# A seven-product form for 106 of 370 weight chunks of a decoder layer, with gate and up as one unit

## The chip, the cores and the metric

The kernel runs on one core of one Trainium2 chip. The metric is the time of one execution on the device in microseconds (us), the median of several runs. The engines are named as in the profile: PE is the matrix engine (PEld its weight loads), DVE the vector engine, ACT the scalar engine, POOL GpSimd, and SP issues the transfers.

## The reference

One decoder layer on 256 tokens of 2048 channels, in float32, with two SwiGLU feed-forwards of inner width 5632 around a mixer and an attention to a memory of 256 rows:

```
h = h + 0.5 * (silu(n @ w1_gate) * (n @ w1_up)) @ w1_down      n = rmsnorm(h) * g_ffn1
z = (rmsnorm(h) * g_mix) @ w_in                                 # 3072 columns, and 256 for keys and values
y = [rmsnorm(spatial gating of z), rmsnorm(attention over a window of 128)]
h = h + y @ w_out
h = h + (attention of 4 heads of 512 to rmsnorm(mem)) @ w_xo    # w_xq, w_xkv
h = h + 0.5 * (silu(n @ w2_gate) * (n @ w2_up)) @ w2_down
out = rmsnorm(h) * g_final
```

## The kernel before

Nearly all of the work is products of the 256 tokens' activations with weights that are streamed once. Tokens lie in two blocks of 128 (tb). A float32 operand is written as a sum of two values of the type float32r, hi + lo, and a product is the sum of three matmuls, hi·hi + hi·lo + lo·hi, into one PSUM bank.

**A chunk** of weights is 1 MB: [128, 4, 512], four 128-row tiles of a 512-column block. `unit` goes over the chunks of one block of 512 columns: SP loads `raw` (three buffers), ACT casts it to `wh`, DVE computes `wl = raw - wh` (two buffers each; `split`, L144 and L145), and PE runs 4 row tiles x 2 token blocks x 3 matmuls (L223 to L225) into two banks of the pool `acc`. The activations are the stationary operand (a transposed [128, 128] block, hi or lo), the weights are the moving one. There are 370 chunks (368 of this form, and two of 256 columns for keys and values).

**A feed-forward** (`ffn`) goes in three phases over 4, 4 and 3 of the 11 blocks of 512 inner columns. For each block there is a gate unit and an up unit (4 chunks each), then silu on ACT (L238), the product on DVE (L240), eight transposes on PE (L162) and the split of the result; after a phase come four down units, one for each 512 columns of h, which are added to h (L251). `next_norm` squares each finished block of h, transposes it and splits it with the next norm's gain (L138, L139); the token's factor rs is applied to the product's rows. The first norm's input comes transposed from the host (xT); x itself is loaded into h later, beside the first block.

**The other stages**: w_in by blocks of 512 columns, window attention (small matmuls) beside the memory's value units, the memory's key units, w_out, then for each head a w_xq unit and its attention, and w_xo. The order of instructions on each engine is made by the tile framework from priorities in the order of the program and from its estimate of when each is ready; an engine then runs its list in order, with semaphores.

Of the kernel before, what the change touches and what calls it, by code (L numbers as in the profile page):

```python
# [30 lines left out]
def layer_kernel(  # L31
# [82 lines left out]
    def rstd_of(parts, n, width, nt=TB):  # L114
        """(mean of squares + eps) ** -0.5 from parts [P, nt, n]."""
        ss = tiny.tile([P, nt], F32, tag="ss", name=nm("ss"))
        if n > 1:
# [6 lines left out]
        nc.gpsimd.tensor_tensor(rs, ms, mhalf[:, :nt], ALU.pow)
        return rs
# [25 lines left out]
    def group_from_rows(s, src, gcol=None, into=None):  # L151
        """Transposed (hi, lo) of 512 columns; src(tb, i) is the [P, 128] block i."""
        if into is None:
            hi, lo = pair(s)
        else:
            hi, lo = [into(s).rearrange("p (k t) -> p k t", k=4) for _ in range(2)]
        for half in range(2):
            ps = bank(s)
            pv = ps.rearrange("p (k t) -> p k t", k=2)
            for i in range(2):  # L160
                for tb in range(TB):
                    nc.tensor.transpose(  # L162
                        pv[:, i, tb * P:(tb + 1) * P], src(tb, 2 * half + i), ident
                    )
# [26 lines left out]
    def unit(s, w, cb, groups, order=None, r0=0, fills=None, apart=False):
# [6 lines left out]
        kt = w.shape[3]  # L198
        ncol = w.shape[4]
        n = len(groups) * 4 // kt  # L200
        ps = [acc.tile([P, 512], F32, tag="acc", name=nm(s)) for _ in range(TB)]
        for at, ci in enumerate(range(n) if order is None else order):
            raw = stream.tile([P, kt, ncol], F32, tag="raw", name=nm(s + "w"), bufs=3)
            wh = stream.tile([P, kt, ncol], F32R, tag="wh", name=nm(s + "wh"))
            wl = stream.tile([P, kt, ncol], F32R, tag="wl", name=nm(s + "wl"))
            step = kt if fills is None else 1 if at == 0 else 2
            for k in range(0, kt, step):
                ks = slice(k, k + step)
                if fills is not None:
                    fills[ci](k, step)  # L210
                nc.sync.dma_start(raw[:, ks, :], w[r0 + ci, cb, :, ks, :])
                split(wh[:, ks, :], wl[:, ks, :], raw[:, ks, :])
            steps = [(k, tb) for k in range(kt) for tb in range(TB)]
            if apart and at == n - 1:
                steps.sort(key=lambda step: step[1])
            for k, tb in steps:
                hi, lo = groups[(ci * kt + k) // 4]
                kg = k % 4
                sl = slice(tb * P, (tb + 1) * P)
                o = ps[tb][:, :ncol]  # L220
                first = at == 0 and k == 0
                last = at == n - 1 and k == kt - 1
                nc.tensor.matmul(o, hi[:, kg, sl], wh[:, k, :], start=first, stop=False)  # L223
                nc.tensor.matmul(o, hi[:, kg, sl], wl[:, k, :], start=False, stop=False)  # L224
                nc.tensor.matmul(o, lo[:, kg, sl], wh[:, k, :], start=False, stop=last)  # L225
        return ps

    def ffn(s, groups, rs, wg, wu, wd, on_block, fills=None, apart=False):
        for p0, p1 in ((0, 4), (4, 8), (8, 11)):
            acts = []  # L230
            for c in range(p0, p1):
                pg = unit(s + "g", wg, c, groups, fills=None if c else fills)
                pu = unit(s + "u", wu, c, groups)
                if callable(rs):
                    rs = rs()
                sg = [s2("sg") for _ in range(TB)]
                for tb in range(TB):
                    nc.scalar.activation(sg[tb], pg[tb], AF.Silu, scale=rs[:, tb:tb + 1])  # L238
# [447 lines left out]
```

## Time and profile before

| what | value |
|---|---|
| runs | 2148.64, 2148.91, 2149.71 us (median 2148.91) |
| profiled execution | span 2147.1 us; the runs' median is 1.8 us more, which lies around the span |
| PE / DVE / ACT busy | 2132.2 / 1074.0 / 903.5 us |
| read from HBM | 398.52 MB, 187 GB/s over the span |
| granted TensorE clock | 0.999 |

Busy shares say how full an engine is, not what bounds; that is read from waits and from the chain that ended last. Matmuls overlap in the pipeline, so a matmul's own duration (some 390 ns) is longer than the distance of two starts.

### The profile page before, as it was taken

To read this page: it belongs to the slowest core of one execution; us is meant where nothing else is said; L and a number is where in the kernel's file an instruction comes from. 1 tells how busy PE (TensorE), PEld (TensorE's weight loads), DVE (VectorE), ACT (ScalarE), POOL (GpSimd) and SP (SyncE) were. 2 spreads that over 40 slices of the span, in tenths; PEclk is the share of its full clock that TensorE was granted. 3 is DMA by queue.
4 is the path that set the end of the run, shared out by engine and by line. 5 is a ranking of instruction groups with operands and counts; after the bars stand their busy time and mean duration, and the time that the engine had idled before them with its cause. 6 is when DMAs were issued, how large, how long until landed. Compare 5 with 4: busy or idle time off the path is not lost.

```text
span 2147.1 us, 22925 instructions
## 1 busy us (share of the span) xinstructions
PE 2132.2 (99%) x9782; PEld 1758.0 (82%) x9782; DVE 1074.0 (50%) x827; ACT 903.5 (42%) x841; POOL 16.7 (1%) x34
## 2 busy tenths in 40 slices
PE   9999999999999999999999999999999999999998
PEld 7888888888888888877888888888888888888886
DVE  5444444454445545555545555545444444544454
ACT  6333333333334455444434454443333343333333
POOL 0000000000000000000000000000000000000000
PEclk9999999999999999999999999999999999999999
DMA  8555555555555575434555534555555555555553
GB/s 296 194 192 184 195 194 190 184 194 196 196 179 195 191 251 202 162 116 157 176 187 186 178 143 169 176 194 184 191 191 190 190 193 188 187 194 196 186 188 136
DMA packets 61398, 402.10 MB, mean 187 GB/s; under 512 B 6752, under 2 KB 10864, under 8 KB 14192
## 3 DMA queue, kind: packets, MB, share of 16 engines
q1 hardware_dynamic: 60048, 396.44, 52.3%
q0 software_dynamic: 1248, 4.20, 0.6%
q8 instruction: 76, 1.25, 0.2%
q14 instruction: 26, 0.21, 0.0%
HBM read 398.52 MB, written 2.10 MB: 187 GB/s over the span
## 4 chain that ended last, share of the span: by engine, by line
PE 96%; DVE 1%; ACT 1%; DMA 1%; issue 0%; SPq 0%; POOL 0%; POOLq 0%; DVEq 0%; ACTq 0%
PE f2g L223 4%; PE f2u L224 4%; PE f2g L224 4%; PE f1d L223 4%; PE f2g L225 4%; PE f1d L225 4%; PE f1d L224 4%; PE f2u L223 4%; PE f2u L225 4%; PE f2d L223 4%; PE f2d L224 4%; PE f2d L225 4%; PE f1g L224 4%; PE f1g L225 4%; PE f1g L223 4%; PE f1u L225 4%
## 5 line engine op out<-in xcount | busy, mean ns | idle before, releaser
L145 DVE TENSOR_TENSOR f2uwl<-f2uw,f2uwh 128x2048 fp32r<-128x2048 f32 x44 | 100.9, 2293 | 138.6 <-ACT f2uwh L144 138.6
L145 DVE TENSOR_TENSOR f1uwl<-f1uw,f1uwh 128x2048 fp32r<-128x2048 f32 x44 | 100.9, 2293 | 138.0 <-ACT f1uwh L144 138.0
L145 DVE TENSOR_TENSOR f2gwl<-f2gw,f2gwh 128x2048 fp32r<-128x2048 f32 x44 | 100.9, 2293 | 114.2 <-ACT f2gwh L144 114.2
L145 DVE TENSOR_TENSOR f1dwl<-f1dw,f1dwh 128x2048 fp32r<-128x2048 f32 x44 | 100.9, 2293 | 112.5 <-ACT f1dwh L144 112.5
L145 DVE TENSOR_TENSOR f2dwl<-f2dw,f2dwh 128x2048 fp32r<-128x2048 f32 x44 | 100.9, 2293 | 111.2 <-ACT f2dwh L144 111.2
L145 DVE TENSOR_TENSOR f1gwl<-f1gw,f1gwh 128x2048 fp32r<-128x2048 f32 (+2 forms) x50 | 101.8, 2036 | 108.7 <-ACT f1gwh L144 108.5
L144 ACT CAST f2gwh<-f2gw 128x2048 fp32r<-128x2048 f32 x44 | 84.1, 1912 | 152.4 <-PE f2g L225 74.8
L144 ACT CAST f2dwh<-f2dw 128x2048 fp32r<-128x2048 f32 x44 | 84.2, 1913 | 151.5 <-PE f2d L225 123.3
L144 ACT CAST f1dwh<-f1dw 128x2048 fp32r<-128x2048 f32 x44 | 84.1, 1912 | 147.3 <-PE f1d L225 126.1
L144 ACT CAST f1gwh<-f1gw 128x2048 fp32r<-128x2048 f32 (+2 forms) x50 | 85.3, 1705 | 139.8 <-PE f1g L225 70.4
L224 PE MATMUL f1g<-f1gwl,n1h 128*128 128x512 f32 x352 | 138.1, 392 | 0.6 <-DVE f1gwl L145 0.5
L223 PE MATMUL f1g<-f1gwh,n1h 128*128 128x512 f32 x352 | 136.6, 390 | 1.8 <-ACT f1gwh L144 1.8
L224 PE MATMUL f2g<-f2gwl,n4h 128*128 128x512 f32 x352 | 137.9, 392 | 0.0
L225 PE MATMUL f1g<-f1gwh,n1l 128*128 128x512 f32 x352 | 137.7, 391 | 0.0
L225 PE MATMUL f2g<-f2gwh,n4l 128*128 128x512 f32 x352 | 137.7, 391 | 0.0
L224 PE MATMUL f1d<-f1dwl,f1ah 128*128 128x512 f32 x352 | 137.5, 391 | 0.0
L223 PE MATMUL f1d<-f1dwh,f1ah 128*128 128x512 f32 x352 | 137.3, 390 | 0.0
L225 PE MATMUL f1d<-f1dwh,f1al 128*128 128x512 f32 x352 | 137.3, 390 | 0.0
L224 PE MATMUL f2d<-f2dwl,f2ah 128*128 128x512 f32 x352 | 137.3, 390 | 0.0
L223 PE MATMUL f2g<-f2gwh,n4h 128*128 128x512 f32 x352 | 137.2, 390 | 0.0
L225 PE MATMUL f2d<-f2dwh,f2al 128*128 128x512 f32 x352 | 137.2, 390 | 0.0
L224 PE MATMUL f2u<-f2uwl,n4h 128*128 128x512 f32 x352 | 137.1, 389 | 0.0
(249 smaller groups left out, 4838.2 us busy)
## 6 DMA issues: line engine op xcount, KB each, us to landing
f1uw<-in_w_up SPq DMA_DIRECT2D x44, 1024.0 KB, 4.8
f1dw<-in_w_down SPq DMA_DIRECT2D x44, 1024.0 KB, 4.8
f2gw<-in_w_gate SPq DMA_DIRECT2D x44, 1024.0 KB, 4.8
f2uw<-in_w_up SPq DMA_DIRECT2D x44, 1024.0 KB, 4.8
f2dw<-in_w_down SPq DMA_DIRECT2D x44, 1024.0 KB, 4.8
f1gw<-in_w_gate SPq DMA_DIRECT2D x40, 1024.0 KB, 4.8
mvw<-in_w_xkv SPq DMA_DIRECT2D x16, 1024.0 KB, 4.8
mkw<-in_w_xkv SPq DMA_DIRECT2D x16, 1024.0 KB, 4.8
```

What stands on the lines that cost most here:

```text
L144: nc.scalar.copy(hi, src)
L145: nc.vector.tensor_tensor(lo, src, hi.bitcast(F32), ALU.subtract)
L223: nc.tensor.matmul(o, hi[:, kg, sl], wh[:, k, :], start=first, stop=False)
L224: nc.tensor.matmul(o, hi[:, kg, sl], wl[:, k, :], start=False, stop=False)
L225: nc.tensor.matmul(o, lo[:, kg, sl], wh[:, k, :], start=False, stop=last)
```

## The change

Two changes go together. First, **units are twice as wide**: a chunk is now 256 rows x 1024 columns (two row tiles k, two blocks j of 512 columns: gate and up of the same inner columns, or two neighbouring blocks of another matrix), still 1 MB as [128, 4, 512], and a unit fills four banks, one for each token block and column block. Seen as a product of 2 x 2 blocks, A (token block, row tile) times B (row tile, column block), a chunk takes eight block products of three matmuls. Second, **some chunks take seven** (Winograd's form of Strassen's product). There are three kinds of activation pair:

- N: eight plain products (mixer, memory);
- C: eight products, but into the sums that the seven-product form uses (banks P2, Q5, Q3, Q4), with two extra activation blocks S3 and S5;
- S: seven products, with sums S1 to S4 of activation blocks and T1 to T4 of weight blocks, into those banks and three more (P1, Q6, Q7, from the pool of transposes).

In a unit that mixes C and S, the results follow from the seven banks by DVE additions: one part after the last S chunk (`early`), one at the end. Kinds by chunk: CCSCSCSC for gate|up (11 units a feed-forward), w_out and w_xo (2 units each), CCSCSCSC CCSCCSC CCSCCSC for the 22 row pairs of down. That makes 106 S chunks; the other units (w_in, w_xq, w_xkv) use N.

`ffn` now runs all 11 gate|up units, keeps their 22 transposed results unsplit, and then runs down in four pieces: half 0 with pairs 0 to 7, half 1 with 0 to 14, half 0 with 8 to 21, half 1 with 15 to 21 (a half is 1024 columns of h). Sums and splits of a pair (`fill_sums`) are made when down first uses it. The first norm now comes from x: loaded in blocks of 512 columns, squared, scaled by an estimate of the factor from the first block, transposed on PE, and filled (`pre1`); the fourth norm is scaled by an estimate from half of h in the same way. Pairs have five slots for C and three for S.

```diff
@@ activations: a pair of row tiles
+    NAMES = {"N": ("A11", "A21", "A12", "A22"),
+        "C": ("A11", "A12", "A21", "A22", "S3", "S5"),
+        "S": ("A11", "A22", "A12", "S3", "S1", "S2", "S4")}
...
+    def fill_sums(s, p, raw):
+        f = s2(s + "f").rearrange("p (k t) -> p k t", k=4)
+        if p.kind == "C":
+            f = f[:, :2, :]
+            nc.vector.tensor_tensor(f, raw[:, 0:2, :], raw[:, 2:4, :], ALU.subtract)
+            split(p.hi[:, :4, :], p.lo[:, :4, :], raw)
+            split(p.hi[:, 4:, :], p.lo[:, 4:, :], f)
         else:
+            nc.vector.tensor_tensor(
+                f[:, 0:2, :], raw[:, 0:1, :].to_broadcast([P, 2, P]), raw[:, 1:3, :], ALU.subtract)
+            split(p.hi[:, :3, :], p.lo[:, :3, :], raw[:, 1:, :])
+            nc.vector.tensor_tensor(f[:, 2, :], raw[:, 1, :], f[:, 1, :], ALU.subtract)
+            nc.vector.tensor_tensor(f[:, 3, :], raw[:, 3, :], f[:, 2, :], ALU.subtract)
+            split(p.hi[:, 3:, :], p.lo[:, 3:, :], f)
@@ products of a chunk
+    MIXED = (("P2", ("A11", "B11"), ("A12", "B21")), ("Q5", ("A21", "B12"), ("A22", "B22")),
+        ("Q3", ("S3", "B12"), ("S5", "B22")), ("Q4", ("A21", "B11"), ("A22", "B21")))
+    SEVEN = (("P1", ("A11", "B11")), ("P2", ("A12", "B21")), ("Q3", ("S4", "B22")),
+        ("Q5", ("S1", "T1")), ("Q7", ("S3", "T3")), ("Q6", ("S2", "T2")), ("Q4", ("A22", "T4")))
...
+        def mm(self, name, a, b):
+            if name not in self.banks:
+                pool, tag = (trp, "tr") if name in ("P1", "Q6", "Q7") else (acc, "acc")
+                self.banks[name] = pool.tile([P, 512], F32, tag=tag, name=nm(self.s + name))
+            (ah, al), (bh, bl) = a, b
+            for x, y in ((ah, bh), (al, bh), (ah, bl)):
...
+        def chunk(self, w, p, pieces=False):
+            raw = stream.tile([P, 4, 512], F32, tag="raw", name=nm(s + "w"), bufs=3)
+            wh = stream.tile([P, 4, 512], F32R, tag="wh", name=nm(s + "wh"))
+            wl = stream.tile([P, 4, 512], F32R, tag="wl", name=nm(s + "wl"))
+            if p.kind == "S":
+                nc.sync.dma_start(raw, w)
+                t = stream.tile([P, 4, 512], F32, tag="t", name=nm(s + "t"), bufs=1)
+                th = stream.tile([P, 4, 512], F32R, tag="th", name=nm(s + "th"), bufs=1)
+                tl = stream.tile([P, 4, 512], F32R, tag="tl", name=nm(s + "tl"), bufs=1)
+                split(wh[:, 1:, :], wl[:, 1:, :], raw[:, 1:, :])
+                nc.vector.tensor_tensor(
+                    t[:, 0:2, :], raw[:, 1:3, :], raw[:, 0:1, :].to_broadcast([P, 2, 512]), ALU.add)
+                nc.vector.tensor_tensor(t[:, 2, :], t[:, 0, :], raw[:, 2, :], ALU.add)
+                nc.vector.tensor_tensor(t[:, 3, :], t[:, 2, :], raw[:, 3, :], ALU.add)
+                split(th, tl, t)
...
+            else:
+                nc.sync.dma_start(raw, w)
+                split(wh, wl, raw)
+            for name, *terms in PRODUCTS[p.kind]:
+                for an, bn in terms:
+                    self.mm(name, p[an], b[bn])
@@ combination (the first early is of gate|up, the second, made by add_early, of down, w_out and w_xo)
+    KINDS = "CCSCSCSC"
+    KINDS_D = "CCSCSCSC" + "CCSCCSC" + "CCSCCSC"
+        def early(u):
+            nc.scalar.copy(p1, u["P1"])
+            nc.vector.tensor_tensor(v, u["Q6"], p1, ALU.subtract)
+            nc.vector.tensor_tensor(z, u["Q7"], v, ALU.add)
...
+        def early(u):
+            nc.scalar.activation(p1, u["P1"], AF.Copy, scale=c)
+            nc.vector.scalar_tensor_tensor(out=v, in0=u["Q6"], scalar=c, in1=p1, op0=ALU.mult, op1=ALU.subtract)
+            nc.vector.scalar_tensor_tensor(out=z, in0=u["Q7"], scalar=c, in1=v, op0=ALU.mult, op1=ALU.add)
+            nc.vector.tensor_tensor(hb[0][0], hb[0][0], p1, ALU.add)
+            nc.vector.tensor_tensor(hb[0][1], hb[0][1], v, ALU.add)
+            nc.vector.tensor_tensor(hb[1][1], hb[1][1], z, ALU.add)
+            nc.vector.tensor_tensor(hb[1][0], hb[1][0], z, ALU.subtract)
+    def add_late(u, c, j0, on_block=None):
+        for name, tb, j in (("P2", 0, 0), ("Q5", 1, 1), ("Q5", 0, 1), ("Q3", 0, 1), ("Q4", 1, 0)):
+            hb = h[:, tb, (j0 + j) * 512:(j0 + j + 1) * 512]
+            nc.vector.scalar_tensor_tensor(out=hb, in0=u[name], scalar=c, in1=hb, op0=ALU.mult, op1=ALU.add)
@@ ffn
+        for c in range(11):
+            got, early = early_of(s + "g")
+            u = mixed_unit(s + "g", wgu, c, n1, early, pre=None if c else pre, first=pre is not None and c == 0)
+            nc.vector.tensor_tensor(p1, u["P2"], p1, ALU.add)
+            nc.scalar.activation(p1, p1, AF.Silu, scale=rs[:, 0:1])
+            nc.vector.tensor_tensor(c22, u["Q5"], z, ALU.add)
+            nc.vector.tensor_tensor(v, u["Q5"], v, ALU.add)
+            nc.vector.tensor_tensor(c12, u["Q3"], v, ALU.add)
+            nc.vector.tensor_tensor(z, u["Q4"], z, ALU.subtract)
+            nc.scalar.activation(z, z, AF.Silu, scale=rs[:, 1:2])
...
+        spans = ((0, 8), (8, 15), (15, 22))
+        for half, parts in ((0, (0,)), (1, (0, 1)), (0, (1, 2)), (1, (2,))):
+            for i in idx:
+                if pairs[i] is None:
+                    pairs[i] = Pair(s + "a", KINDS_D[i])
+                    fill_sums(s + "a", pairs[i], acts[i])
+                u.chunk(wd[i, half], pairs[i])
+                if i == last:
+                    add_early(s + "d", 0.5, 2 * half)(u)
+            add_late(u, 0.5, 2 * half, on_block if 2 in parts else None)
```

More of the change, by code (lines that the diff above doesn't have):

```diff
@@ L191, in unit @@
[L191 to L226, printed above, removed]
@@ new lines, in transposed, with row_tile, pair_from_rows @@
+    def transposed(s, kind, src):
+        ps = bank(s).rearrange("p (k t) -> p k t", k=4)
+        for i, (k, tb) in enumerate(LAID[kind]):
+            nc.tensor.transpose(ps[:, i, :], src(tb, k), ident)
+        return ps
+    def row_tile(kind, v, k):
+        return v[:, k::2, :] if kind == "C" else v[:, 2 * k:2 * k + 2, :]
+    def pair_from_rows(s, kind, src, gcol, slot=None):
+        ps = transposed(s, kind, src)
+        p = Pair(s, kind, slot)
+        if kind == "N":
+            for k in range(2):
+                g = sm[:, gcol + k:gcol + k + 1]
+                split_scaled(row_tile("N", p.hi, k), row_tile("N", p.lo, k), row_tile("N", ps, k), g)
+            return p
+        raw = s2(s + "r").rearrange("p (k t) -> p k t", k=4)
+        for k in range(2):
+            g = sm[:, gcol + k:gcol + k + 1]
+            nc.scalar.activation(row_tile(kind, raw, k), row_tile(kind, ps, k), AF.Copy, scale=g)
+        fill_sums(s, p, raw)
+        return p
@@ new lines, in mixed_unit @@
+    def mixed_unit(s, w, cb, pairs, early, pre=None, first=False):
+        u = Unit(s, [p.kind for p in pairs] if pre is None else KINDS)
+        last = max(i for i, k in enumerate(u.kinds) if k == "S")
+        for i in range(len(u.kinds)):
+            if pre is not None:
+                pre(i)
+            u.chunk(w[i, cb], pairs[i], pieces=first and i < 2)
+            if i == last:
+                early(u)
+        return u
+    KINDS = "CCSCSCSC"
+    KINDS_D = "CCSCSCSC" + "CCSCCSC" + "CCSCCSC"
@@ L286, in layer_kernel, with scaled @@
-    parts2, n2, on2 = next_norm("n2", G_MIX)
-    ffn("f1", n1, rs1, w1_gate, w1_up, w1_down, on2, fills=[m[1] for m in made])
-    rs2 = rstd_of(parts2, NG, D)
+            if j < 2:
+                if done[0] + done[1] < 2 * TB:
+                    return
+                st["est"] = rstd_of(parts[:, :, :2], 2, 1024)
+                for i in range(2):
+                    scaled(i)
+            elif done[j] == TB:
+                scaled(j)
+        def scaled(j):
+            r = [s2(s + "s") for _ in range(TB)]
+            for tb in range(TB):
+                nc.scalar.activation(
+                    r[tb], h[:, tb, j * 512:(j + 1) * 512], AF.Copy, scale=st["est"][:, tb:tb + 1]
+                )
+            make(j, lambda tb, c: r[tb][:, c - j * 512:c - j * 512 + P])
@@ L504, in split4, with rows_scaled, transposed4 @@
         return hi, lo
-    def transposed4(s, src):
+    def rows_scaled(s, ps, rs):
+        out_ = [[s2(s) for _ in range(TB)] for _ in range(2)]
+        for name, tb, j in BLOCKS:
+            nc.scalar.activation(out_[j][tb], ps[tb, j], AF.Copy, scale=rs[:, tb:tb + 1])
+        return out_
+    def transposed4(s, rows_):
         flat = m4(s)
@@ new lines, in layer_kernel @@
+    partsb = tiny.tile([P, TB, 2], F32, tag="partsb", name="partsb")
+    for tb in range(TB):
+        for j in range(2):
+            square_into(partsb[:, tb, j:j + 1], yb[tb][:, j * 512:(j + 1) * 512], 512)
+    ny = scaled_pairs("ya", ya, partsa, G_Y, 0) + scaled_pairs("yb", yb, partsb, G_Y + 8, 4)
+    n3, on3, rs3_ = next_norm("n3", G_X)
+    for cb in range(2):
+        u = mixed_unit("wo", w_out, cb, ny, add_early("wo", 1.0, 2 * cb))
+        add_late(u, 1.0, 2 * cb, on3)
+    rs3 = rs3_()
```

507 lines of the change are left out of this document (316 added, 191 removed), and 3 rows, old and new, of the table LAID.

## The prediction

> **What bounds the kernel now.** I read the page first (busy time, chain), then who waits on PE, then one steady unit by windows and by timeline.
>
> ```profile
> span 2147.1 us, 22925 instructions
> PE 2132.2 (99%) x9782; PEld 1758.0 (82%) x9782; DVE 1074.0 (50%) x827; ACT 903.5 (42%) x841; POOL 16.7 (1%) x34
> PE 96%; DVE 1%; ACT 1%; DMA 1%; issue 0%; SPq 0%; POOL 0%; POOLq 0%; DVEq 0%; ACTq 0%
> ```
>
> ```profile
> PE f1g L223 <- ACT f1gwh L144: 1.8, 2, 1.2
> PE f1g L224 <- DVE f1gwl L145: 0.5, 1, 0.5
> ```
>
> ```profile
> 96.50:140.96 44.46, 44.46 (x201) 36.82 (x200) 20.96 (x13) 17.53 (x12) 0.00 (x0) 1.00 0.52 189
> ```
>
> ```profile
> 301.01 1.91 ACT L144 CAST f1uwh<-f1uw 128x2048 fp32r<-128x2048 f32 x1 [2.94 <-PE f1u L225]
> 306.45 1.91 ACT L144 CAST f1uwh<-f1uw 128x2048 fp32r<-128x2048 f32 x1 [3.53 <-PE f1u L225]
> ```
>
> ```profile
> 302.95 2.29 DVE L145 TENSOR_TENSOR f1uwl<-f1uw,f1uwh 128x2048 fp32r<-128x2048 f32 x1 [3.15 <-ACT f1uwh L144]
> ```
>
> PE is the chain (96%), and hardly waits: the two longest waits of PE on another engine after the warm-up sum to 2.3 us. In the steady unit (one gate and one up block, 8 chunks) PE is busy for all of its 44.46 us at full granted clock, DVE for 20.96. The casts of the high parts start 5.44 us apart, because each waits until PE has left the chunk two before it (wh and wl have two buffers): a chunk of 24 matmuls is 5.44 us, one matmul 5.44/24 = 0.2267 us. DVE then waits 3.15 us for that cast. So a matmul less is worth 0.2267 us as long as DVE, half idle today, can take what is put on it.
>
> **Matmuls: -72.1 us.** A chunk of kind C still has 8 products of 3 matmuls (24), one of kind S has 7 (21). S chunks: 22 gate|up units with 3 each (66), two downs with 14 each (28), w_out and w_xo with 2 units of 3 each (12): 106. 106 x 3 x 0.2267 = 72.1. The number of weight loads falls alike, and so does nothing else: weight bytes and chunk sizes (1 MB) are as before.
>
> **Prices on DVE and ACT.** These rows carry them:
>
> ```profile
> L145 DVE TENSOR_TENSOR f1uwl<-f1uw,f1uwh 128x2048 fp32r<-128x2048 f32 x44 | 100.9, 2293 | 138.0 <-ACT f1uwh L144 138.0
> L145 DVE TENSOR_TENSOR f1gwl<-f1gw,f1gwh 128x1024 fp32r<-128x1024 f32 x6 | 7.3, 1224 | 1.5 <-ACT f1gwh L144 1.3
> L145 DVE TENSOR_TENSOR f1gwl<-f1gw,f1gwh 128x512 fp32r<-128x512 f32 x4 | 2.8, 693 | 2.2 <-ACT f1gwh L144 2.2
> L251 DVE SCALAR_TENSOR_TENSOR h<-f1d,h 128x512 f32<-128x512 f32 x24 | 16.5, 692 | 6.1 <-PE f1d L225 6.1
> L240 DVE SCALAR_TENSOR_TENSOR sg<-f1u,rs,sg 128x512 f32<-128x512 f32 x22 | 15.7, 750 | 5.2 <-PE f1u L225 5.2
> L139 DVE SCALAR_TENSOR_TENSOR n1l<-n1r,sm,n1h 128x256 fp32r<-128x256 f32 x16 | 7.2, 479 | 3.0 <-ACT n1h L138 3.0
> L388 DVE SCALAR_TENSOR_TENSOR u<-sv,sm,u 128x128 f32<-128x128 f32 x16 | 4.3, 344 | 4.3 <-PE sv L381 4.3
> ```
>
> ```profile
> L144 ACT CAST f1uwh<-f1uw 128x2048 fp32r<-128x2048 f32 x44 | 84.2, 1913 | 110.0 <-PE f1u L225 69.3 <-PE f1g L225 37.8 <-DMA f1uw<-in_w_up 3.0
> L144 ACT CAST f1gwh<-f1gw 128x1024 fp32r<-128x1024 f32 x6 | 6.3, 1051 | 1.6 <-DMA f1gw<-in_w_gate 1.5
> L238 ACT ACTIVATE sg<-f1g,rs 128x512 f32<-128x512 f32 x22 | 15.0, 687 | 28.5 <-PE f1g L225 28.5
> ```
>
> Missing widths lie on the line through 512 and 1024 elements (1.037 ns an element and 162 ns): 128 gives 0.295 us (344 ns above, another operation), 256 gives 0.428 (479 above), 384 gives 0.56; 1536 lies between 1224 and 2293, by proportion 1.755, on ACT 1.482. Then, on DVE:
> - a C chunk: 2.29, as now;
> - an S chunk: wl of three slots 1.755, T1 and T3 1.224, T2 and T4 0.693 each, tl 2.293, together 6.66; on ACT 1.482 + 1.913;
> - sums and low parts of one activation pair (fill_sums): C 0.428 + 0.693 + 0.428 = 1.55, S 0.428 + 0.56 + 2 x 0.295 + 0.693 = 2.27;
> - a gate|up unit's combination: v, z, and the five late adds 7 x 0.692, the two products by up 2 x 0.75, together 6.34; down, w_out and w_xo: add_early 6 x 0.692 = 4.15, add_late 5 x 0.692 = 3.46.
>
> **Gate|up, 21 units after the first: +4 us.** PE: 183 matmuls x 0.2267 = 41.5, and the 0.95 of transposes that 44.46 - 8 x 5.44 leaves: 42.4. DVE: 5 x 2.29 + 3 x 6.66 + 6.34 = 37.8, that is 89%. ACT: 5 x 1.913 + 3 x 3.395 + 5 x about 0.69 = 23. So PE stays the longest, and the question is the order of arrival. Tightest is the C chunk behind an S: its wh slot is free when the S begins, the S takes only 21 x 0.2267 = 4.76, and cast and low part take 0.2 (the gap between release and cast) + 1.91 + 2.29 = 4.4; the low part is used by the third matmul, 0.45 later, so 0.8 is spare. A T sum (up to 1.22) already running on DVE can eat that and cost 0.4. For the S chunk, wh is free after the nine matmuls of P1, P2 and Q3 of the S before; th and tl (one buffer) are free when that S ends, and are needed 5.44 + 9 x 0.2267 + 0.45 = 7.9 later: th 1.91 and tl 2.29 leave 3.7. Between 0 and 3 x 0.4 = 1.2 a unit (0 to 25 us); I take 0.2, since only a badly placed sum costs. The four banks P2, Q5, Q3, Q4 have no second set any more, but the last C chunk finishes them 1.36 us apart and the next unit asks for them in the same order at the same distance; one or two adds of 0.69 each fit.
>
> **Down: +16 us.** Per feed-forward, PE 44 x 5.44 - 14 x 0.68 = 229.9. DVE by unit (PE in brackets):
> - half 0, part 0, with all 8 fills new: 31.4 + 14.6 + 7.6 = 53.6 (41.5);
> - half 1, parts 0 and 1: 56.2 + 12.3 + 7.6 = 76.1 (78.2);
> - half 0, parts 1 and 2: 49.6 + 12.3 + 7.6 = 69.5 (73.5);
> - half 1, part 2: 24.8 + 7.6, and 3.8 for the next norm's low parts, 36.2 (36.7).
>
> Here DVE is about as long as PE. In the first unit 4.6 can be done in the idle DVE time of the last gate|up unit (slots come free there one by one) and the 3.46 of late adds slip into the next: 45.5 against 41.5, 4 lost. The other three are 95 to 99% full; I charge 2% of 188, another 4. 8 per feed-forward, between 0 and 27 (DVE kept busy for 90% of the time only).
>
> **w_out, w_xo and into the second feed-forward: +9 us.** A unit is 31.4 + 7.6 = 39 on DVE against 41.5. Added are fills: part of ny in w_out (most lies beside the key units, where DVE is half idle), n3 3.8, xo 7, n4 7 beside w_xo's second unit and 7 beside the first gate|up (45 against 42.4). I charge 1, 2, 3 and 3; between 0 and 20.
>
> **Start: +10 us.** n1 was split straight from xT; now x is loaded, squared, scaled, transposed, copied, summed and split, ahead of the weights on SP's queue.
>
> ```profile
> 6.10 0.73 PE L223 MATMUL f1g<-f1gwh,n1h 128*128 128x512 f32 x2 [1.19 <-ACT f1gwh L144]
> 318.27 0.82 PE L162 MATMUL f1a<-ident,sg 128*128 128x128 f32 x6
> ```
>
> ```profile
> 53.83 0.66 PE f1a L162 x6
> 98.06 0.66 PE f1a L162 x6
> ```
>
> ```profile
> f1gw<-in_w_gate SPq DMA_DIRECT2D x4, 256.0 KB, 4.3
> h<-in_x SPq DMA_DIRECT2D x2, 1024.0 KB, 8.0
> L129 ACT ACTIVATE junk<-h 128x512 f32<-128x512 f32 x40 | 24.8, 623 | 7.2 <-DVE h L251 7.2
> L129 ACT ACTIVATION_READ_ACCUMULATOR junk<-h 128x1 f32 x40 | 7.5, 188 | 0.0
> L138 ACT ACTIVATE n3h<-n,sm 128x256 fp32r<-128x256 f32 x16 | 6.7, 468 | 3.2 <-DVE n3l L139 3.2
> 849.68 0.72 POOL rs L124
> ```
>
> 512 KB of x land between 4.3 and 8.0 us after the issue, say 6, at about 7.3. Then squares 2 x 0.81, mean and power 0.9, two scaled copies 1.38, four transposes 0.55 (0.82 for six), two copies 0.94, a difference 0.43, the cast 0.6: 13.7, instead of 6.10. With 41.5 of matmuls and 28 more transposes (3.8) the first unit ends at 59; before, its transposes came at 53.83, some 1.6 after its end, so 52.2. 59 - 52.2, and the 2.0 that the -72.1 already took from this unit: 8.8. ACT's end is later: 4 x 6.9 of this preparation (squares 1.62, copies 1.38, four copies of 468 ns, casts 2) and 19.75 of casts from 7.3 on, then 2.3 and 5.4 for the last chunk, 62: 12. I take 10.
>
> **Ends and edits without cost.** kv follows halves instead of quarters of h, so four pairs of n2 come at once while kv's first half (some 5.5 us) covers them: +2, between 0 and 5. The last matmuls' block is one [128, 512] in both kernels: +1. Memory attention and mT keep their cover (whole units of 43.5 us). SP's queue issues the same megabytes; the DMA share of 0.52 has room.
>
> **Sum.** -72.1 + 4 + 16 + 9 + 10 + 2 + 1 = -30. The profiled execution's span is 2147.1, the median of the runs 2148.9, 1.8 around it. 2148.9 - 30 = 2119.
>
> **Rivals.**
> - All hidden: DVE totals stay under PE and all waits are nothing but the start's 8.8: 2148.9 - 72.1 + 8.8 = 2086. For it: 89% in the units that hold most S chunks, and today's queues put work where it is ready, as PE does here, with the finished unit's transposes between matmuls of the next. Against: down's 53.6 against 41.5.
>
> ```profile
> 318.03 0.40 PE L223 MATMUL f1g<-f1gwh,n1h 128*128 128x512 f32 x1
> 318.84 0.48 PE L224 MATMUL f1g<-f1gwl,n1h 128*128 128x512 f32 x1
> ```
>
> - Slower, by one hand-over: tl on DVE waits for th on ACT (1.91, and th for the last T sum on DVE), with nothing placed between, so every S chunk idles DVE for about 1.95. Gate|up then needs 43.6 of DVE against 42.4 (25 in all), down 259 against 230 (58), w_out, w_xo and after 46, the start 12, the ends 3: 144, 2221; with half the wait, 66 given back and the 13 of start and ends, 2156. It decides from (72 - 13)/106 = 0.56 us for each S chunk. For it: the 3.15 us that DVE waits in front of each low part, with nothing between. Against: DVE had nothing else to do there. The Trainium skill, page "TensorE: Matmul & The Clock Gate", section "Architectural detail: the array is 16× 32×32, not 1× 128×128", says that VectorE and ScalarE take their queue strictly in order; by that rule the wait is paid wherever the program's order leaves nothing between, this rival's case.
> - PE pauses that cost clock. In the tail PE's last matmul begins before 2138 and the granted clock falls later:
>
> ```profile
> 2138.00:2140.00 2.00, 0.00 (x0) 0.00 (x0) 1.12 (x4) 0.83 (x3) 0.00 (x0) 1.00 0.95 347
> 2140.00:2142.00 2.00, 0.00 (x0) 0.00 (x0) 1.27 (x4) 0.72 (x1) 0.55 (x1) 0.76 0.49 177
> 2142.00:2144.00 2.00, 0.00 (x0) 0.00 (x0) 0.06 (x1) 0.00 (x0) 0.00 (x0) 0.50 0.95 344
> ```
>
> More than 2 us without a matmul pass at clock 1.00, and half of it is granted by 2142. My longest pause is about 2 us; if three (two downs, the start) grew past 4, each would run a chunk at half clock, 3 x 5.4 = 16: 2135. The Trainium skill, same page ("TensorE: Matmul & The Clock Gate"), section "Why this matters for your kernels", puts the limit at gaps of about 3 us; the rows above agree as far as they go, and the sum is the same by both as long as pauses stay short.
> - That the matmuls don't go away can't be: the loops fix their number.
>
> **How the numbers follow.** Mine 0.60 (own range 2098 to 2140), all hidden 0.17, slower 0.19 (2140 to 2221), clock 0.04. A change of 0.2% (4.3 us) is about what a measurement of this kernel tells from none. Faster: 0.57 + 0.17 + 0.03 = 0.77; within 0.2%: 0.03 + 0.01 + 0.02 = 0.06; slower 0.17. The range runs from just under the all-hidden case to the half-wait case with a little room: 2083 to 2160; some 0.05 lie below, 0.13 above.
>
> **What would show it.** PE matmuls fewer by 318 less 32 new transposes; a gate|up unit of 42.4 to 42.7 us instead of 44.46; DVE near 1800 us busy; waits of PE on tl or wl of down's first unit, of some 4 us a feed-forward; the first unit's transposes near 62. Wrong would be: PE waits behind tl in nearly every S chunk (the slower rival), or DVE sums that take longer than the widths' line says, T1/T3 with its broadcast operand above all, which no row shows.

## The result, and the profile after

The changed kernel takes 2163.11 us (median of 4 runs, 2162.19 to 2165.49) against 2148.77 (2148.45 to 2149.71) for the kernel before: ratio 1.0068, 95% interval 1.0054 to 1.0082. It is slower, and 44 us from the 2119 forecast. The span and the busy times of the page after, and the engines' shares of the chain that ended last:

```profile
span 2161.0 us, 23831 instructions
PE 2095.2 (97%) x9496; PEld 1710.1 (79%) x9496; DVE 1691.8 (78%) x1660; ACT 1148.2 (53%) x1163; POOL 25.9 (1%) x36
PE 85%; DVE 7%; ACT 4%; issue 2%; POOL 0%; DMA 0%; SPq 0%; POOLq 0%; DVEq 0%; ACTq 0%
```

The matmuls did go: 9782 - 9496 = 286 = 318 less 32 new transposes. But PE is no longer the whole chain: 85% instead of 96%. Two steady gate|up units of the first feed-forward, then three windows in the first down (columns: window, its length, busy PE, PEld, DVE, ACT, POOL, granted clock, DMA share, GB/s):

```profile
81.00:123.30 42.30, 42.30 (x192) 35.03 (x191) 36.32 (x31) 22.37 (x16) 0.00 (x0) 1.00 0.54 198
123.30:165.60 42.30, 42.30 (x192) 35.02 (x191) 35.74 (x30) 22.46 (x16) 0.00 (x0) 1.00 0.53 199
505.00:527.00 22.00, 21.07 (x95) 16.63 (x93) 21.68 (x28) 13.12 (x13) 0.00 (x0) 1.00 0.46 159
527.00:549.00 22.00, 19.06 (x79) 14.42 (x80) 20.93 (x24) 8.64 (x8) 0.00 (x0) 1.00 0.61 223
549.00:590.00 41.00, 41.00 (x180) 33.45 (x181) 40.60 (x46) 25.14 (x24) 0.00 (x0) 1.00 0.52 179
```

A gate|up unit takes 42.30 us instead of 44.46 with PE never idle and DVE 6 us short of full: there the change does what it says. In these windows of down DVE is busy 21.68 of 22.00 us and 40.60 of 41.00, and PE begins to pause. DVE is that full only there. These are the four pieces of the first down, each as a whole:

```profile
500.60:548.40 47.80, 43.93 (x193) 34.41 (x191) 46.42 (x58) 25.48 (x24) 0.00 (x0) 1.00 0.54 195
548.40:630.80 82.40, 79.70 (x345) 64.49 (x346) 72.11 (x75) 42.58 (x36) 0.00 (x0) 1.00 0.54 191
630.80:708.00 77.20, 75.31 (x325) 61.84 (x324) 64.28 (x66) 39.39 (x35) 0.00 (x0) 0.98 0.52 191
708.00:746.60 38.60, 38.60 (x179) 31.84 (x177) 32.19 (x33) 21.34 (x24) 0.00 (x0) 1.00 0.48 171
```

The waits of PE, the longest first (us in all, times, longest):

```profile
PE n L196 <- ACT n1s L529: 5.8, 1, 5.8
PE f1dQ L277 <- ACT f1ah L136: 5.2, 3, 1.9
PE f2dQ L277 <- ACT f2ah L136: 5.2, 3, 1.9
PE n L196 <- ACT n1r L214: 4.1, 2, 2.1
PE f1gP L277 <- ACT n1h L136: 3.4, 2, 2.2
PE f2dQ L277 <- ACT f2dth L136: 2.3, 3, 1.1
PE f1dQ L277 <- ACT f1dth L136: 2.3, 3, 1.1
PE woQ L277 <- ACT woth L136: 1.9, 2, 1.1
```

No single wait carries the loss, so I summed PE's lost time by place: the distance between the starts of neighbouring matmuls less 0.2268, 0.122 or 0.118 us (512, 256 or 128 columns), over the whole trace. That counts waits and half-clock matmuls (below) alike. By its four pieces the 13.9 of the first down are 5.3, 4.2, 3.7 and 0.7.

| place (us of the span) | before | after |
|---|---|---|
| start, 0 to 100 | 5.4 | 27.0 |
| first down, 500 to 750 | 0 | 13.9 |
| mixer and memory values, 750 to 1000 | 12.5 | 15.0 |
| w_out, w_xq, w_xo, 1000 to 1400 | 1.6 | 22.6 |
| into f2 and its gate\|up, 1400 to 1900 | 0.2 | 7.7 |
| second down, 1900 on | 0 | 12.0 |

With 0.5 at 450 to 500 that is 80 us more lost time. -72.1 of matmuls + 3.8 of transposes + 80 + 2.5 after the last matmul (13.2 instead of 10.7) gives 14, the difference of the spans (2161.0 - 2147.1 = 13.9). The 72 us of matmuls are saved, and the pauses cost more than that.

### The profile page after: what moved, and what is told of

The parts are those of the page before. It is cut to its first block, busy times and chain, and to the rows that moved or that the text cites. A ratio compares the mean times of both kernels' runs of the same rounds, so it can differ in the third digit from the quotient of the medians.

```text
span 2161.0 us, 23831 instructions
## 1 busy us (share of the span) xinstructions
PE 2095.2 (97%) x9496; PEld 1710.1 (79%) x9496; DVE 1691.8 (78%) x1660; ACT 1148.2 (53%) x1163; POOL 25.9 (1%) x36
## 4 chain that ended last, share of the span: by engine, by line
PE 85%; DVE 7%; ACT 4%; issue 2%; POOL 0%; DMA 0%; SPq 0%; POOLq 0%; DVEq 0%; ACTq 0%
PE f1gQ L277 15%; PE f2gQ L277 14%; PE f1dQ L277 6%; PE f2dQ L277 6%; PE f1gP L277 6%; PE f2gP L277 5%; PE mv L277 4%; PE mk L277 4%; PE xq L277 4%; PE f1dP L277 2%; PE f2dP L277 2%; PE v L277 2%; PE q L277 2%; PE xoQ L277 2%; PE u L277 2%
## 5 line engine op out<-in xcount | busy, mean ns | idle before, releaser
L136 ACT CAST f1gwh<-f1gw 128x1536 fp32r<-128x1536 f32 (+2 forms) x94 | 155.3, 1653 | 97.1 <-PE f1gQ L277 75.0
L137 DVE TENSOR_TENSOR f1gwl<-f1gw,f1gwh 128x1536 fp32r<-128x1536 f32 (+2 forms) x94 | 182.8, 1966 | 20.6 <-ACT f1gwh L136 20.2
L137 DVE TENSOR_TENSOR f2gwl<-f2gw,f2gwh 128x1536 fp32r<-128x1536 f32 (+1 forms) x88 | 182.0, 2087 | 7.6 <-ACT f2gwh L136 6.9
L136 ACT CAST f2gwh<-f2gw 128x1536 fp32r<-128x1536 f32 (+1 forms) x88 | 153.1, 1750 | 61.0 <-PE f2gQ L277 32.7
L277 PE MATMUL f1gQ<-f1gwh,n1h 128*128 128x512 f32 x363 | 142.1, 392 | 0.0
L277 PE MATMUL f1gQ<-f1gwh,n1l 128*128 128x512 f32 x363 | 142.0, 391 | 0.0
L277 PE MATMUL f2gQ<-f2gwh,n4l 128*128 128x512 f32 x363 | 141.9, 391 | 0.0
L277 PE MATMUL f1gQ<-f1gwl,n1h 128*128 128x512 f32 x363 | 141.8, 391 | 0.0
L277 PE MATMUL f2gQ<-f2gwh,n4h 128*128 128x512 f32 x363 | 141.5, 390 | 0.0
L277 PE MATMUL f2gQ<-f2gwl,n4h 128*128 128x512 f32 x363 | 141.2, 390 | 0.0
L137 DVE TENSOR_TENSOR f2dwl<-f2dw,f2dwh 128x2048 fp32r<-128x2048 f32 (+1 forms) x44 | 92.5, 2116 | 15.9 <-ACT f2dwh L136 15.6
L277 PEld LDWEIGHTS f1gQ<-f1gwh,n1h 128*128 128x128 f32 x363 | 68.9, 190 | 14.7
```

Source lines behind the costliest of these rows:

```text
L136: nc.scalar.copy(hi, src)
L137: nc.vector.tensor_tensor(lo, src, hi.bitcast(F32), ALU.subtract)
L277: nc.tensor.matmul(self.banks[name], x, y, start=name not in self.begun, stop=self.left[name] == 0)
```

## The experiments

Theories at the outset: ORDER (work is issued too late: it stands behind other work in the program) and LOAD (the sums fill DVE and ACT). Times are medians; the kernel before took 2148.4 to 2148.8 beside them. "Lost" is PE's lost time as above.

**Where the seven products pay: e1, e2, e7.** The edits put plain pairs in all chunks (e1), in all but gate|up (e2), in w_out and w_xo alone (e7); shapes and order of the units stay. The code here and below is shortened.

```
-    KINDS_D = "CCSCSCSC" + "CCSCCSC" + "CCSCCSC"      # e1, e2; w_out and w_xo likewise
+    KINDS_D = "N" * 22
```

> All 370 chunks with eight products (kind N everywhere: no activation or weight sums, no combination), everything else as in the changed kernel: wide units, gate and up as one, whole gate|up and then whole down, the first norm from x. Theory ORDER: the 80 us of new PE pauses come from work that the program issues too late (preparation of the next unit stands behind the matmuls of this one), whatever DVE's load. Then the pauses of the start (22) and at the stage changes (some 10) stay, and the time is 2148.8 + 3.8 (32 transposes) + 32 to 36 = 2185 to 2190. Theory LOAD: the pauses come from what the sums put on DVE and ACT. Then only the start's first chain (8) is left: 2148.8 + 3.8 + 8 = 2161.

> S chunks only in the 22 gate|up units (66 of 106); down, w_out and w_xo with eight plain products and no sums. Against e1_plain this adds 66 x 3 matmuls less (44.9 us), and pauses of about 4 in gate|up. ORDER: 2185 - 41 = 2144 to 2149. LOAD: 2161 - 41 = 2120, and some 8 more if the first unit's sums add to the start. Against the changed kernel it gives up 40 x 0.68 = 27 us of matmuls and loses the pauses of down and w_out/w_xo that come from sums (at most 50).

> Seven products in the gate|up and down units; w_out and w_xo take plain chunks (12 seven-product chunks fewer, 36 matmuls or 8.2 us more than the changed kernel). LOAD (VectorE is full in the pieces of down that also fill pairs: busy 21.68 of 22.00 us and 40.60 of 41.00 in the changed kernel): down pauses as there, about 26 us in both, against 19.1 us of matmuls saved, so slower than with gate|up alone: 2143.6 - 19.1 + 26 = about 2150, and w_out and w_xo carry the other 13 us to 2163. Rival ELSEWHERE (down pays, and w_out and w_xo alone lose): 2143.6 - 19 + 5 = about 2130.

| seven products in | us | ratio to before, interval | step | matmuls of the step |
|---|---|---|---|---|
| nothing (e1) | 2171.8 | 1.0108, 1.0091 to 1.0125 | | |
| gate\|up (e2) | 2143.6 | 0.9978, 0.9969 to 0.9987 | -28.2 | -44.9 |
| and down (e7) | 2153.4 | 1.0021, 1.0012 to 1.0031 | +9.8 | -19.1 |
| and w_out, w_xo (changed) | 2163.1 | 1.0068, 1.0054 to 1.0082 | +9.7 | -8.2 |

Without sums (e1) down, w_out, w_xo and gate|up lose almost nothing; 17.3 us are lost at the start and 3.8 in front of w_out. So the layout alone costs 23 us, 16 of them at the start (11.9 of pauses more than before, 3.8 of transposes), and the sums bring the other pauses. e1's time lies between the forecasts (LOAD 2161, ORDER 2185 to 2190). e2 comes out beside ORDER's 2144, but by luck: that number starts from e1's 2185, which was not met, and counts 41 us for a step of 28. e7 is near LOAD's 2150 and far from ELSEWHERE's 2130. Only gate|up pays. In e2's down, without sums, DVE is far from full, and PE never stops:

```profile
527.00:549.00 22.00, 22.00 (x99) 18.22 (x98) 11.89 (x9) 7.65 (x4) 0.00 (x0) 1.00 0.55 192
549.00:590.00 41.00, 41.00 (x183) 33.94 (x182) 20.78 (x15) 18.19 (x15) 0.00 (x0) 1.00 0.53 188
```

**Order of the issue: e3, e4.** e3 issues the next x block's preparation behind a chunk instead of ahead of its own. e4 adds: down's fills two chunks ahead, the four sums of add_early behind the late ones, and w_out's pairs between the last key unit's chunks.

```
+            if pre is not None and i == 0:
+                pre(0)
             u.chunk(w[i, cb], pairs[i], pieces=first and i < 2)
+            if pre is not None and i % 2 == 0 and i + 2 < 8:
+                pre(i + 2)
```

> The changed kernel, but the preparation of the next two pairs of the first norm (load of x, squares, scaling, transposes, sums) is issued right behind chunk i instead of right before chunk i + 2, so it ranks ahead of chunk i + 1's matmuls. Same work. ORDER: the three pauses before the second to fourth block of x (2.3, 2.2 and 2.2 us, each with another 1 for the low parts and the half-clock stretch behind it, together some 14) go: 2163 - 14 = 2149. LOAD: ACT and DVE are full in the first unit, so at most 4 go: 2159.

> The changed kernel with the same work issued earlier in four places: the start as in e3_start_ahead; the sums and splits of down's pairs two chunks ahead of their use; in down's first two pieces the four sums into h behind the last chunk's additions, which free the banks; the pairs of w_out between the chunks of the last key unit. ORDER: start 14, down's pauses at piece changes (about 8 a feed-forward), the 4.8 before w_out: 2163 - 35 = 2128. LOAD: the start's 4 and little else: 2155 to 2160.

e3: 2153.0 (ratio 1.0019, 1.0010 to 1.0028); the start loses 15.8 instead of 27. ORDER holds for 11 us of the start. e4: 2145.9 (0.9988, 0.9978 to 0.9997), between ORDER's 2128 and LOAD's 2155 to 2160. The two downs lose 9.1 and 9.4 us instead of 13.9 and 12.0: the waits where a piece of down ends went, those on the cast of the sums grew (in the first down from 2.3 us in three places to 4.3 in five). The wait on the memory keys moved to 4.9 us in one place, and w_out and w_xo kept theirs.

**Load on DVE: e8, e9.** e8 moves the sums of weights to POOL; e9 leaves out the low parts of the weights of the chunks without seven products in down, w_out and w_xo, so it is a test of the load and no kernel to use.

```
-                nc.vector.tensor_tensor(t[:, 2, :], t[:, 0, :], raw[:, 2, :], ALU.add)   # e8, the other two too
+                nc.gpsimd.tensor_tensor(t[:, 2, :], t[:, 0, :], raw[:, 2, :], ALU.add)
-                split(wh, wl, raw)                                                       # e9
+                nc.scalar.copy(wh, raw); wl = wh
```

> The changed kernel with one edit: the three sums of weights of each seven-product chunk (1024, 512 and 512 columns) run on GpSimd instead of VectorE, which takes 2.6 us of VectorE from each of the 106 chunks, about 275 us in all. LOAD (VectorE's fill in down, w_out and w_xo makes the pauses): the pauses of down fall from 26 to about 5 us and those of w_out, w_xq and w_xo from 26 to about 12, the start stays: about 2163 - 35 = 2128. Rival HAND-OVER (PE waits for the cast of the sums, which waits for the sums, however free VectorE is): GpSimd's sums come later than VectorE's, the waits for the cast of the sums grow and spread to gate|up: 2165 to 2200.

> The changed kernel, but the low parts of the weights of the chunks that do not take the seven products in down, w_out and w_xo are left out (the matmuls read the high part in their place): 80 subtractions of 2288 ns, 183 us of VectorE, go, and every matmul and the whole chain of the seven-product chunks stay. LOAD (VectorE has no room left in the pieces that fill pairs): down's pauses fall from 26 to under 5 us, and of the 26 us in w_out, w_xq and w_xo only those behind the memory keys and in the attention of the memory stay (about 12): 2163 - 33 = about 2130. Rival HAND-OVER (sums, cast, subtraction, matmul of one chunk stand in a row whatever else VectorE does): the waits for the cast of the sums stay, only the piece changes gain: about 2155.

e8: 2336.2 (1.0869, 1.0850 to 1.0888), far above both forecasts. It doesn't decide: POOL is slow, and DVE slows with it. Steady gate|up units, 166 to 460 us (line, engine, operation, out<-in, shapes, count | busy, mean ns | idle before). The changed kernel's DVE:

```profile
L137 DVE TENSOR_TENSOR f1gwl<-f1gw,f1gwh 128x1536 fp32r<-128x1536 f32 x21 | 36.8, 1753 | 3.3 <-ACT f1gwh L136 3.3
L294 DVE TENSOR_TENSOR f1gt<-f1gw 128x1024 f32<-128x1024 f32 x21 | 25.7, 1222 | 0.5
```

e8, DVE and POOL:

```profile
L137 DVE TENSOR_TENSOR f1gwl<-f1gw,f1gwh 128x1536 fp32r<-128x1536 f32 x19 | 44.3, 2330 | 0.4
...
L294 POOL TENSOR_TENSOR f1gt<-f1gw 128x1024 f32<-128x1024 f32 x20 | 59.2, 2961 | 147.1 <-DMA f1gw<-in_w_gu 84.0 <-DVE f1gtl L137 63.0
```

e9: 2124.0 (0.9885, 0.9870 to 0.9900). Matmuls and the seven-product chunks' own steps are those of the changed kernel, and 39 us go: down's 13.9 and 12.0 fall to 1.7 and 0.3, w_out to w_xo from 22.6 to 14.7, f2's gate|up from 7.7 to 1.5. The same windows of down, in e9:

```profile
505.00:527.00 22.00, 22.00 (x98) 18.21 (x97) 20.30 (x28) 14.54 (x13) 0.00 (x0) 1.00 0.51 180
527.00:549.00 22.00, 22.00 (x98) 17.93 (x97) 16.32 (x27) 10.91 (x8) 0.00 (x0) 1.00 0.59 213
549.00:590.00 41.00, 41.00 (x183) 33.94 (x182) 28.57 (x32) 25.05 (x26) 0.00 (x0) 1.00 0.54 191
```

LOAD is shown for down: with room on DVE (82% busy in the first piece instead of 97%, 58 to 64% instead of 83 to 88% in the others), the same chain of sums, cast and subtraction hardly makes PE wait, in the same order of work. The edit also spares the other chunks' matmuls their wait for low parts; in the changed kernel's first down one such wait, of 1.0 us, stands out. e4 shows that the order has a part beside it: with the same load it took away 7.4 of down's 25.9 us.

**The start, with seven products in gate|up only: e5, e6, e10, e11.** e5 is e2 with e3's edit; e6 fills the first pairs from the transposed x, as the kernel before did; e10 is e6 with `pre` two chunks ahead; e11 is e5 with `WARM = 20`.

> Seven products in the 22 gate|up units only (down, w_out and w_xo take plain chunks), and the first norm's next x block is issued right behind the chunk before it instead of ahead of its own chunk. ORDER (the start's pauses come from work that stands too late in program order): the start's pauses shrink as they did in the changed kernel with this edit, from 27.6 to about 16 us, and nothing else moves: 2143.6 - 11.6 = about 2132. Rival CLOCK (what the start gains is lost again to half-clock stretches later): 2138 to 2143.

> Seven products in the 22 gate|up units only, and the first norm's pairs made from the transposed x in DRAM as the kernel before did (no squares, no estimate, no scaled rows, no 32 transposes on the way; the row scale is made behind the first unit). CHAIN (the start is late because of the new chain x, square, estimate, scaled rows, transposes, scaled copies, cast): the first real matmul comes near 7 us, the start's pauses fall from 27.6 to 5 to 8 us and the 32 transposes (3.8 us) go: 2143.6 - 20 - 4 = about 2120. Rival FILL (the start is late because the casts and sums of the first chunks fill ScalarE and VectorE, wherever x comes from): pauses stay near 15 to 18 us, 2130.

> Seven products in gate|up only, first pairs from the transposed x as in e6_gate_xT, and each pair's load and work issued two chunks ahead. ORDER (e6's pauses of 3.81 and 6.62 us at 50 and 61 us are loads and casts that stand behind later weights in the queue: the last load of x was issued at 51.02 us): start's pauses fall from 25 to about 8 us: 2136.6 - 17 = about 2120. Rival FILL (VectorE and ScalarE are short of time in the first 60 us whatever the order): 2130 to 2137.

> e5_gate_ahead with 20 warm-up matmuls instead of 9, so that PE works on until about 10.5 us, where the first transposes begin. CLOCK (the pause of 5 us there makes PE run at half clock in the 9 us behind it: 0.53 in 11 to 20 us): that stretch runs at full clock and some 18 matmuls take 0.227 instead of 0.425 us: 2133.0 - 3.6 = about 2129.5. Rival CHAIN (what comes next waits for casts anyway, so that a faster clock only waits longer): 2132 to 2134.

| | us | ratio to before, interval | lost, 0 to 100 us |
|---|---|---|---|
| e5 | 2133.0 | 0.9927, 0.9912 to 0.9942 | 16.0 |
| e6 | 2136.6 | 0.9944, 0.9927 to 0.9960 | 25.5 |
| e10 | 2129.1 | 0.9906, 0.9889 to 0.9922 | 16.5 |
| e11 | 2133.1 | 0.9925, 0.9910 to 0.9940 | 13.3 |

e5 meets ORDER's number. The time of e6 misses both of its forecasts: the first matmul came at 7.3 us, but 3.8 and 6.6 us were lost at 50 and 61 us, behind casts and a load of x issued at 51.02. e10, with them ahead, gains 7.6 of the 17 that ORDER asked for and lies just under FILL's 2130 to 2137, so it meets neither. Its start loses as much as e5's; both transposed-x kernels save the 32 transposes too, and that is e10's 3.9 us over e5. e11: the pause in front of the first transposes shrank from 5.3 to 3.4 us, the wait behind them grew from 1.1 to 1.7, and the time stayed, as CHAIN said. It is no test of CLOCK, though: the granted clock from 11 to 20 us rose only from 0.53 to 0.62, so most of that stretch kept its half clock.

**What is left of the start: e12, e13, e17, e18.** In e10 PE still waits three times for the cast of the sums. ACT's timeline there:

```profile
46.68 1.91 ACT L137 CAST f1gwh<-f1gw 128x2048 fp32r<-128x2048 f32 x1 [0.90 <-PE f1gQ L280]
48.49 0.90 ACT L538 ACTIVATE n1r<-n1t,sm 128x256 f32<-128x256 f32 x2
49.30 1.88 ACT L137 CAST f1gth<-f1gt 128x2048 fp32r<-128x2048 f32 x1
```

ACT stands at the next chunk's cast until PE frees a buffer, and the cast that PE needs (f1gth) is behind it. e12 takes DVE work away (it leaves out the low parts of the weights of chunks 3, 5 and 7 of the first unit, so it and e17 are tests and no kernels to use), e13 orders ACT, e17 does both, e18 is e13 with x's residual loads behind the unit's weights.

```
-        nc.scalar.copy(hi, src)                                   # e13: casts of wh after an S chunk
+        with tc.issue_after(behind.ins):
+            cast = nc.scalar.copy(hi, src)
```

> e10_xT_ahead, but in the first unit the low parts of the weights of chunks 3, 5 and 7 are left out (the matmuls read the high part in their place): 3 x 2.29 = 6.9 us less on VectorE before 62 us, all else as it was. FILL (what is left of the start's pauses is VectorE, which has to fill pairs, split weights and form the sums at once: busy 67.07 of 75 us in 6 to 81 us in e10): the pauses of 2.49, 2.49 and 1.59 us at 36.8, 51.2 and 62.6 us go, 2129.1 - 6 = about 2123. Rival HAND-OVER (sums, cast, matmul in a row within one seven-product chunk, as the wait for the cast of the sums says): they stay, 2128 to 2130.

> e10_xT_ahead with one edit: on ScalarE the cast of a chunk's high parts is queued behind the cast of the sums of the seven-product chunk before it (in e10 four of 66 stand the other way round: three in the first unit and one in the second feed-forward). QUEUE (ScalarE stands at a cast that waits for PE to free a buffer, and the cast of the sums that PE needs is behind it): the pauses of 0.75, 2.49 and 2.49 us at 24.9, 36.8 and 51.2 us go: 2129.1 - 5.5 = about 2123.5. Rival CHAIN (the sums, their cast and the matmul follow each other too closely whatever the order): 2128 to 2130.

> e13_queue_gate and e12_start_no_wl in one: on ScalarE the cast of a chunk's high parts behind the cast of the sums before it, and the low parts of the weights of chunks 3, 5 and 7 of the first unit left out (the matmuls read the high part). TWO IN TURN (ScalarE's order and VectorE's load each make the same wait, and whichever is taken away leaves the other): the start's pauses fall from 20.8 us to about 12, 2133.7 - 8 = about 2125. Rival LOADS (the arrival of the loads sets them): 2131 to 2134.

> e13_queue_gate with the two loads of x for the residual (2 MB in all) queued behind the last load of the first unit's weights; in e13 they are issued in the middle of it, and ScalarE waits 1.38 and 1.25 us for pieces of the transposed x at 30.5 and 35.1 us. LOADS: the pauses of 2.00, 1.85 and 3.18 us at 38, 52 and 65 us shrink by 3 to 5 us: about 2129.5. TWO IN TURN: 2132 to 2135.

Lost at the start: e10 16.5, e12 18.4, e13 20.8, e18 19.3, e17 10.7 us; times 2129.1, 2130.5 (ratio 0.9913, 0.9896 to 0.9929), 2133.7 (0.9928, 0.9911 to 0.9944), 2133.6 (0.9934, 0.9918 to 0.9951) and 2125.2 (0.9893, 0.9879 to 0.9908). Either edit alone gains nothing (e13 comes out 4.6 us above e10); both together gain 8 us over e13 and 4 over e10, as TWO IN TURN said, though the intervals of e17 and e10 overlap. Later loads of x do nothing (e18, for which LOADS asked 2129.5). The lost times here are of one profile each, and e12's four runs alone lie from 2128.5 to 2133.3, so a difference of 2 to 4 us between two starts is not shown. In e13 the cast is in front and waits for DVE's sums instead:

```profile
49.26 0.69 DVE L305 TENSOR_TENSOR f1gt<-f1gt,f1gw 128x512 f32<-128x512 f32 x1
```

```profile
49.99 1.90 ACT L138 CAST f1gth<-f1gt 128x2048 fp32r<-128x2048 f32 x1 [0.48 <-DVE f1gt L305]
```

**The same order in the whole kernel: e14, e15, e16.** e14 is the changed kernel with e13's edit; e15 and e16 add the start of e10 and e4's late sums in down, e15 with seven products in gate|up and down, e16 in all.

> The changed kernel with the same one edit (there 11 of 106 stand the other way round: 3 in each down, 2 in w_out, 2 in w_xo, 1 in the second gate|up). QUEUE: the pauses on the cast of the sums go (0.78, 0.77 and 1.23 us in each down, 1.25 and 0.92 in w_out, 0.77 in w_xo, 0.77 in f2): about 9 us, 2163.1 - 9 = 2154. Rival DVE (VectorE is full there, 21.68 of 22.00 us, and what does not wait for ScalarE will wait for VectorE's parts): 2159 to 2164.

> Seven products in gate|up and down, none in w_out and w_xo; first pairs from the transposed x two chunks ahead, the order on ScalarE of e13, and the four sums into h at the end of down's first two pieces put behind the late ones. ORDER (what down lost, it lost by the order of work): down's pauses fall from 26 to under 10 us against 19.1 us of matmuls: e13 (2123.5) - 9 = about 2115. DVE (VectorE is full while down fills pairs): pauses near 20 us, no better than e13 without the seven products in down: 2122 to 2126.

> All 106 chunks in seven products, with the edits of e15. ORDER: w_out and w_xo give back some of their 8.2 us of matmuls: about 2112 to 2116. DVE: as in the changed kernel they cost about 10 us more than they save: e15 + 10, that is 2125 to 2135.

2176.5 (1.0126, 1.0111 to 1.0141), 2140.0 (0.9964, 0.9951 to 0.9977) and 2159.0 (1.0046, 1.0031 to 1.0061): worse than the rivals named. In e14's first down the cast of the sums, now in front, waits 6.32 us for DVE, which is as full as it was:

```profile
526.09 1.90 ACT L137 CAST f1dth<-f1dt 128x2048 fp32r<-128x2048 f32 x1 [6.32 <-DVE f1dt L302]
```

```profile
505.00:527.00 22.00, 20.92 (x95) 16.67 (x93) 21.88 (x32) 10.83 (x12) 0.00 (x0) 1.00 0.41 144
```

In the changed kernel this cast began at 525.34, without a wait. The first piece of each down then loses 9.1 us instead of 5.3 and 5.4, and w_out to w_xo 27.2 instead of 22.6. So my QUEUE theory falls: the tile framework's order, with 11 of 106 casts behind the next chunk's, was the better one here. e15 is 6 us slower than e13, with 19.1 us of matmuls less; e16 is another 19 slower. Of the versions that leave nothing out, the one to take is e10: 2129.1 us, 0.9% under the kernel before.

## Why the prediction was wrong

- **Matmuls, -72.1**: right (318 fewer), and so were DVE's prices: 1536 wide 1753 ns (forecast 1755), T1 and T3 1222 (1224).
- **Gate|up, +4**: right in size, and in part by luck. The steady unit is 42.30 us (forecast 42.4 and 0.2 of pauses in every unit); f1's lose 0.5 in all (450 to 500 us), f2's about 4.4 (1450 to 1900 us), so 4.9.
- **Down, +16**: mis-sized, 25.9. The step that failed is "95 to 99% full; I charge 2%": how full DVE is over a unit did not set what PE lost. The first piece lost 5.3 and 5.4 us against 4 charged, with DVE 97% full. The other three lost 8.6 and 6.6 against 4 charged, and there DVE was busy for 72.1 of 82.4 us, 64.3 of 77.2 and 32.2 of 38.6, that is 83 to 88% and less than forecast: with a full queue DVE's additions of 0.69 us start 0.60 us apart (at 626 us), so a sum of durations counts too much. They lost mostly by the order of DVE's queue: near the end of the first three pieces DVE did the four sums into h ahead of the last chunk's difference, and PE waited 1.5 to 1.9 us each time for the cast behind it, with a stretch at half clock behind one of the three. Moving that work (e4) or taking load off DVE (e9) took these waits away.
- **w_out, w_xo and into f2, +9**: mis-sized most, with the start. 21.0 from 1000 to 1400 us and 3.0 from 1400 to 1450, so 24. I counted DVE's total by unit, where it stays under PE, and not the stretches. e7, without sums in w_out and w_xo, loses 7.0 there, so 15.6 of the 22.6 come with the sums, and e9 takes 8 of them away with DVE's load; what makes the rest is not split.
- **Start, +10**: 25.4 (21.6 of pauses, 3.8 of transposes). I added up one chain to the first matmul (13.7 us, 14.50 came) and took ACT's total for the rest. That each later block's chain would also be exposed, because its transposes stand behind the chunk before, I did not see: 11 us (e3), at waits of some 2.2 us that each brought half clock. The sums have a part in the same time: without them, in the same late order, the start loses 17.3 instead of 27.0 (e1). The first unit's transposes came at 81.2 us instead of near 62.
- **Ends, +3**: 5 (2.5 in the mixer's stretch, 2.5 after the last matmul).

Errors of 9.9 in down, 15 in w_out to f2, 15.4 at the start, 2 at the ends and 1 in gate|up make the 44 us, but for rounding. The rival "one hand-over" forecast the sign but not the mechanism. DVE does idle in front of tl in gate|up:

```profile
L137 DVE TENSOR_TENSOR f2gtl<-f2gt,f2gth 128x2048 fp32r<-128x2048 f32 x33 | 75.7, 2292 | 56.8 <-ACT f2gth L136 54.7
L137 DVE TENSOR_TENSOR f1gtl<-f1gt,f1gth 128x2048 fp32r<-128x2048 f32 x33 | 75.7, 2293 | 53.0 <-ACT f1gth L136 53.0
```

53.0/33 = 1.6 us for each S chunk, 4.8 a unit, which the unit's 6 us of spare DVE time cover. In down it waits so for 8.0 us, 0.6 for each S chunk, a third as long. The rival on the clock was put at pauses past 4 us, and pauses of 2 us were enough (below). "All hidden" failed where DVE has no spare time or does other work first.

## What to carry to other kernels

Trade matmuls for vector work stage by stage: a stage paid here only where PE hardly waited for the sums (gate|up, DVE busy for 36 of 42 us), and not where DVE was full (21.7 of 22). A low busy share is not enough: down's later pieces had DVE 83 to 88% busy, as gate|up has, and lost time near their ends, where DVE did other work ahead of what PE needed. When an engine that runs its list in order is full, moving a late instruction forward can make another late: e14 lost 13 us so, while e4's moves gained 7. What gained was to take work off it (e9) or to take the change out of that stage (e2). And prepare the second operand of the next chunk ahead of the current chunk's matmuls: e3 and e5 each gained 10 us by that.

## What was not expected of the hardware

A pause of PE of 2 us already halved the granted clock behind it. After the wait of 2.06 us for n1r that ended at 46.94, in the changed kernel:

```profile
45.00:46.90 1.90, 0.00 (x0) 0.00 (x0) 1.87 (x3) 1.88 (x3) 0.00 (x0) 1.00 0.15 60
46.90:48.50 1.60, 1.56 (x6) 1.47 (x7) 1.60 (x2) 0.93 (x3) 0.00 (x0) 0.52 0.01 5
48.50:50.50 2.00, 2.00 (x5) 1.09 (x5) 2.00 (x6) 1.97 (x6) 0.00 (x0) 0.53 0.43 78
50.50:52.50 2.00, 2.00 (x11) 1.61 (x10) 1.70 (x7) 2.00 (x6) 0.00 (x0) 1.00 1.04 442
...
630.70:632.70 2.00, 2.00 (x6) 1.51 (x6) 1.58 (x4) 0.88 (x1) 0.00 (x0) 0.50 0.01 4
706.50:708.50 2.00, 1.98 (x9) 1.68 (x10) 2.00 (x5) 1.46 (x5) 0.00 (x0) 1.00 0.45 188
```

Clock 0.52 for some 3.5 us, 5 matmuls in 2 us instead of 9, then 1.00. The wait of 1.9 us before 706.5, at a piece change of down, had no such stretch behind it, though one just as long, before 629.3, had. From the tail before I had read that more than 2 us pass at full clock. The Trainium skill, page "TensorE: Matmul & The Clock Gate", section "Why this matters for your kernels", puts the limit at gaps of about 3 us; this trace shows less.

The clock records of this trace show a grid. From 33 us to the last matmul half clock begins at 33.32, 46.98, 64.04, 630.66, 1118.76 and 2033.53 us, each time for 3.41 us, and these times lie 4, 5, 166, 143 and 268 times 3.413 us apart. Cut into windows on that grid, the pause that ended at 629.3 lies in one window, 2.0 us of it idle, and half clock follows; the one before 706.5 lies across a border at 705.75, 1.3 and 0.8 us idle, and none follows. So here the idle time within such a window goes with the half clock behind it, and not the length of one pause; that it decides is inferred, and the bound isn't sharp, since a window with 1.97 us idle (from 1429.4 us) had none.

POOL and DVE slow each other: in the steady gate|up units of e8, with POOL adding beside it, a DVE subtraction of 1536 columns took 2330 ns in the mean instead of 1753. In e8 as a whole it took 1753 ns (median) where no addition of POOL ran beside it, and 2841 where one did all the time; POOL's additions of 512 columns took 1297 ns with DVE idle and 2685 with DVE busy beside them.
